# Every engine's queue of a two-layer decoder trunk in an order that a walk over the traced program fixes

## The chip, the cores and the metric

The kernel runs on one core of one Trainium2 chip. The core has several engines that each work through a queue of their own: TensorE (PE) multiplies matrices and transposes, VectorE (DVE) and ScalarE (ACT) work element by element, SyncE (SP) issues most of the DMAs, GpSimd (POOL) does nothing here that counts. An instruction waits at the head of its queue until what it depends on has signalled; what is queued behind it on the same engine waits too. Times are device microseconds (us), and lower is better.

## The reference, cut to what matters

`x` is 256 tokens by 2048. Layer 0 mixes tokens by four causal trailing means (windows 2, 4, 8, 16) with a 512x512 weight for each quarter of the columns; layer 1 by differential attention with 8 heads. Each mixer is followed by a SwiGLU feed-forward part with 5632 inner columns.

```python
for i in range(DEPTH):                       # 2 layers
    hn = rmsnorm(h, norm_mix[i])
    mix = pool_mixer(...) if i % 2 == 0 else diff_attention(...)
    h = h + mix
    h = h + swiglu(rmsnorm(h, norm_ffn[i]), w_gate[i], w_up[i], w_down[i])
return rmsnorm(h, final_norm)

def swiglu(h, wg, wu, wd):
    return (jax.nn.silu(h @ wg) * (h @ wu)) @ wd
```

In the attention a head has two softmaxes, `a = p[0] - lam * p[1]`, and its output `a @ v` is normalised once more before `w_o`.

## The kernel before, in words

All matrices are float32, and each factor of a large product is split in a high and a low part that PE multiplies in its float32r form: high by high, high by low, low by high. `halves` (L118) makes the two parts of a weight tile of four 512-column blocks: `whi` on ACT (L124) and `wlo` on DVE (L125). The weights come by DMAs of 1 MB each, issued by SP (L115), into 3 buffers `raw`; `whi` and `wlo` have 3 buffers each, so the cast to a new `whi` can start only when PE is through with the one three tiles earlier.

The products are made in *groups*. A group takes 8 steps (in w_down 2n of them, n the feed-forward groups of a chunk), one for each pair of 128-row slices of the weight, and sums them in PSUM banks `b0` to `b7`. A plain step makes four blocks of the output with eight products; a *seven* step makes the same with seven products, as in Strassen's and Winograd's scheme, and needs sums of weight blocks (`tsum`, L130 to L133, DVE) and their high and low parts `thi` (L139, ACT) and `tlo` (L140, DVE), as well as sums of the activations (L272 to L277). Steps 2, 4 and 6 are seven steps in most groups. `combined` (L204 to L221) then forms the four output blocks from the banks: copies on ACT (L210, L214) and eight DVE instructions on tiles `c` (L211, L212, L213, L215 to L218, L220), several of which need the one ahead:

```python
nc.vector.tensor_tensor(u2, ps[M6], m1, ALU.add)      # L211
nc.vector.tensor_tensor(u3, ps[M7], u2, ALU.add)      # L213
nc.vector.tensor_tensor(u2, p5, u2, ALU.subtract)     # L215
nc.vector.tensor_tensor(p5, p5, u3, ALU.subtract)     # L216
nc.vector.tensor_tensor(u2, ps[P3], u2, ALU.add)      # L217
```

The stages, in the order in which the program is written: the layer-0 mixer (pool "start"); a feed-forward part with 11 gate-up groups in chunks of 4, 4 and 3, each chunk followed by 2 groups of w_down; four q-and-k groups of two heads each; two v groups of four heads each; two w_o groups; the second feed-forward part; the last normalisation (`finish`).

Behind a gate-up group, ACT applies silu (L486), DVE multiplies gate and up (L487), PE transposes the result in eight 128x128 pieces (L259), and the transposed blocks become `h`, the left factor of w_down. Behind a q-and-k group, ACT scales the blocks (L551), PE transposes them (L607), makes the scores (L576) and, after the softmax on DVE and ACT (L578 to L592), transposes the probabilities `a_sb` (L561). Behind a v group PE multiplies by the probabilities (L622 to L624), a normalisation follows (squares L628 on ACT, `rsqrt` L229 to L234 on DVE with a square root L230 on ACT, scaling L632), and PE transposes `o_n` (L259).

What sets the order: the tile framework takes instructions in the order of the program, weighed by priorities that the code gives at two places (`high_priority(-100)` for one residual, `high_priority(-LATER)` for the last means of the mixer), and puts each engine's instructions into its queue. Work of the next group is written behind what follows a group, but in PE's queue its first products stand among the transposes.

Of the kernel before, what the change touches and what calls it, by code (L numbers as in the profile page):

```python
# [2 lines left out]

# [11 lines left out]
PSUM = bass.MemoryType.PSUM  # L15
# [10 lines left out]
EPS = 1e-6  # L26
WARM = 8
LATER = 70

WINDOWS = (2, 4, 8, 16)  # L30

# [19 lines left out]

A22, A21, A11, A12, S1, S3, S2, S4 = range(8)
T1, T3, T2, T4 = range(4)


@with_exitstack
def trunk_kernel(ctx, tc, x_n, gains, scale_in, final_in, subln, lam_in, band, counts_in, dist,
# [230 lines left out]
    with tc.tile_pool(name="start", bufs=1, reuse_waits="tile") as st:  # L288
# [81 lines left out]
        def scaled_halves(g):  # L370

            y[g] = [st.tile([P, 2, 512], F32R, name="y_hl", bufs=4) for _ in range(2)]
            for t in range(2):
                split(y[g][t], yp[g][t], r_in[:, t:t + 1])

        def means(g):

            zp[g] = [bank(2 + t) for t in range(2)]
            own = lambda t: band_sb[:, g, t * P:(t + 1) * P]
            for j in range(2):  # L380
                nc.tensor.matmul(zp[g][0], own(0), y[g][0][:, j], start=(j == 0), stop=(j == 1))
            for j in range(2):
                nc.tensor.matmul(zp[g][1], own(1), y[g][1][:, j], start=(j == 0), stop=False)
            for j in range(2):
                nc.tensor.matmul(zp[g][1], own(2), y[g][0][:, j], start=False, stop=(j == 1))
# [45 lines left out]
        scaled_halves(3)  # L431
        with tc.high_priority(-LATER):
            means(3)
# [94 lines left out]
    with tc.tile_pool(name="attn", bufs=1, reuse_waits="tile") as ap_, ExitStack() as heads:  # L528
        hq = heads.enter_context(tc.tile_pool(name="qk_sums", bufs=1, reuse_waits="tile"))
        at = heads.enter_context(tc.tile_pool(name="attn_tmp", bufs=2, reuse_waits="tile"))  # L530
# [65 lines left out]
        for g in range(4):  # L596

            order, by_seven = LATE if g else EARLY
# [14 lines left out]
        at = heads.enter_context(tc.tile_pool(name="out_tmp", bufs=2, reuse_waits="tile"))  # L613

        oT = [None] * NP
        for g in range(2):
            order, by_seven = LATE if g else EARLY
# [25 lines left out]
                transposed(xq, j, 4, SEVEN)  # L643

    ffn(1, xq, ss_next, None, None)


def _steps(w, left, right):
# [85 lines left out]
```

## Time and profile before

| | us |
|---|---|
| median of 3 runs | 1836.91 (1836.82 to 1837.41) |
| the profiled execution, its own time | 1837.09 |
| its span, first to last instruction | 1835.3 |
| PE busy | 1823.0 of 1835.3 |
| DVE busy | 1630.5 |
| ACT busy | 1048.7 |

The span is what the profile's records cover; the run's own time lies 1.8 us above. "Busy" for PE means that a matmul or transpose was under way; a weight load (PEld) runs beside it. In a row of the timeline, the first number is the start in us from the span's start, the second how long the row's instructions took from the first one's start to the last one's end, then engine, line, operation, the tile written and the tiles read, their shapes, and how many instructions the row stands for (x6); what stands in brackets is idle time of the engine ahead of it and what ended it. A matmul's duration in such a row (0.39) is longer than the distance from one to the next (0.23), since they are pipelined.

### The profile page before, as it was taken

The numbers are of one execution on the slowest core, as the hardware profiler recorded it, in microseconds if no ns is written. First come the engines' busy times: TensorE is split into PE (matmuls) and PEld (weight loads), VectorE is DVE, ScalarE is ACT, GpSimd is POOL, SyncE is SP. The second block draws the span as 40 slices with busy tenths as digits, with TensorE's granted clock in tenths as the row PEclk, the third lists the DMA queues.
The fourth block names the chain that finished last, engine by engine and source line by source line (L and its number), as shares of the span: only waits on it lengthen the run. The fifth ranks groups of instructions, "written<-read, shape, count | busy, mean of one in ns | idle before, by whom it ended". The sixth has DMA issues, their size and how long they took to land.

```text
span 1835.3 us, 20926 instructions
## 1 busy us (share of the span) xinstructions
PE 1823.0 (99%) x8192; PEld 1492.3 (81%) x8192; DVE 1630.5 (89%) x1692; ACT 1048.7 (57%) x1026; POOL 0.7 (0%) x6
## 2 busy tenths in 40 slices
PE   9999999999999999999999999999999999999997
PEld 6888888888888888888888888888888888888886
DVE  7999999889899899989988789889899899988986
ACT  6655544555554556666667665555554555555563
POOL 0000000000000000000000000000000000000000
PEclk9999999999999999999999999999999999999999
DMA  7555555555555555544554555555555545556552
GB/s 271 200 184 193 208 196 209 204 187 205 205 194 197 205 184 184 206 173 174 182 183 163 181 184 184 206 185 205 204 190 202 207 183 193 212 215 210 202 189 110
DMA packets 50930, 356.35 MB, mean 194 GB/s; under 512 B 6160, under 2 KB 6288, under 8 KB 8464
## 3 DMA queue, kind: packets, MB, share of 16 engines
q1 hardware_dynamic: 49968, 353.40, 53.5%
q10 hardware_dynamic: 864, 1.63, 0.2%
q8 instruction: 64, 1.05, 0.2%
q14 instruction: 34, 0.28, 0.0%
HBM read 352.90 MB, written 2.10 MB: 193 GB/s over the span
## 4 chain that ended last, share of the span: by engine, by line
PE 97%; DVE 1%; ACT 1%; DMA 0%; issue 0%; SPq 0%; DVEq 0%; ACTq 0%
PE b L189 93%; PE b L259 2%; PE b L576 1%; PE b L607 0%; DMA x_tok<-x_n 0%; PE b L368 0%; PE b L624 0%; PE b L622 0%; PE b L623 0%; PE b L561 0%; DVE wlo L354 0%; DVE xt_hl L252 0%; ACT sq L240 0%; DVE wlo L125 0%; DVE z L392 0%
## 5 line engine op out<-in xcount | busy, mean ns | idle before, releaser
L189 PE MATMUL b<-whi,xp 128*128 128x512 f32 x2784 | 899.4, 392 | 0.0
L124 ACT CAST whi<-raw 128x1536 fp32r<-128x1536 f32 (+1 forms) x328 | 578.7, 1764 | 549.6 <-PE b L189 450.4
L125 DVE TENSOR_TENSOR wlo<-raw,whi 128x1536 fp32r<-128x1536 f32 (+1 forms) x328 | 689.6, 2103 | 159.2 <-ACT whi L124 158.9
L189 PEld LDWEIGHTS b<-whi,xp 128*128 128x128 f32 x2784 | 520.1, 188 | 108.2 <-ACT e L272 0.4
L189 PE MATMUL b<-wlo,xp 128*128 128x512 f32 x1392 | 544.2, 391 | 0.0
L189 PE MATMUL b<-whi,h 128*128 128x512 f32 x1108 | 354.2, 390 | 0.0
L189 PEld LDWEIGHTS b<-wlo,xp 128*128 128x128 f32 x1392 | 261.5, 188 | 53.0
L140 DVE TENSOR_TENSOR tlo<-tsum,thi 128x2048 fp32r<-128x2048 f32 x114 | 260.6, 2286 | 8.3 <-ACT thi L139 8.3
L189 PEld LDWEIGHTS b<-whi,h 128*128 128x128 f32 x1108 | 207.5, 188 | 43.2
L139 ACT CAST thi<-tsum 128x2048 fp32r<-128x2048 f32 x114 | 217.6, 1908 | 19.7 <-DVE tsum L133 17.2
L189 PE MATMUL b<-thi,xp 128*128 128x512 f32 x640 | 223.4, 389 | 0.0
L189 PE MATMUL b<-wlo,h 128*128 128x512 f32 x554 | 215.8, 389 | 0.0
L130 DVE TENSOR_TENSOR tsum<-raw 128x1024 f32<-128x1024 f32 x114 | 139.1, 1220 | 2.1 <-DMA raw<-w_v 0.6
L189 PEld LDWEIGHTS b<-thi,xp 128*128 128x128 f32 x640 | 120.1, 188 | 24.7
L189 PE MATMUL b<-tlo,xp 128*128 128x512 f32 x320 | 125.9, 393 | 0.0
L189 PEld LDWEIGHTS b<-wlo,h 128*128 128x128 f32 x554 | 104.0, 188 | 21.3
L189 PE MATMUL b<-thi,h 128*128 128x512 f32 x240 | 83.7, 390 | 0.0
L133 DVE TENSOR_TENSOR tsum<-tsum,raw 128x512 f32<-128x512 f32 x114 | 78.5, 689 | 2.2
L132 DVE TENSOR_TENSOR tsum<-tsum,raw 128x512 f32<-128x512 f32 x114 | 78.1, 685 | 0.6
L189 PEld LDWEIGHTS b<-tlo,xp 128*128 128x128 f32 x320 | 60.0, 188 | 16.5 <-DVE tlo L140 4.4
L189 PE MATMUL b<-whi,oT 128*128 128x512 f32 x216 | 69.7, 395 | 0.0
L189 PEld LDWEIGHTS b<-thi,h 128*128 128x128 f32 x240 | 45.0, 188 | 9.5 <-ACT thi L139 0.4
(147 smaller groups left out, 1211.7 us busy)
## 6 DMA issues: line engine op xcount, KB each, us to landing
raw<-w_gu SPq DMA_DIRECT2D x176, 1024.0 KB, 4.8
raw<-w_down SPq DMA_DIRECT2D x88, 1024.0 KB, 4.8
raw<-w_qk SPq DMA_DIRECT2D x32, 1024.0 KB, 4.8
raw<-w_v SPq DMA_DIRECT2D x16, 1024.0 KB, 4.8
raw<-w_o SPq DMA_DIRECT2D x16, 1024.0 KB, 4.8
x_tok<-x_n SPq DMA_DIRECT2D x4, 512.0 KB, 6.9
w<-pool_w SPq DMA_DIRECT2D x4, 512.0 KB, 7.5
raw<-pool_w SPq DMA_DIRECT2D x2, 1024.0 KB, 11.1
```

The source lines that it names most:

```text
L124: nc.scalar.copy(hi[:, lo_block:], raw[:, lo_block:])
L125: nc.vector.tensor_tensor(lo[:, lo_block:], raw[:, lo_block:], f32(hi[:, lo_block:]), ALU.subtract)
L130: nc.vector.tensor_tensor(t[:, T1:T3 + 1], raw[:, B11:B22 + 1], raw[:, B12:B12 + 1].broadcast_to([P, 2, 512]), ALU.add)
L132: nc.vector.tensor_tensor(t[:, T2], t[:, T1], raw[:, B22], ALU.add)
L133: nc.vector.tensor_tensor(t[:, T4], t[:, T2], raw[:, B21], ALU.add)
L139: nc.scalar.copy(hi, t)
L140: nc.vector.tensor_tensor(lo, t, f32(hi), ALU.subtract)
L189: nc.tensor.matmul(ps[b], x, y[:, block], start=first, stop=(left[b] == 0))
L259: nc.tensor.transpose(ps[:, i, 1 - t if seven else t], src(i, t), ident)
L576: nc.tensor.matmul(sc[:, :nk], qk[:, 0, c, qb * P:(qb + 1) * P], qk[:, 1, c, :nk], start=True, stop=True)
```

## The change

At the end of `trunk_kernel`, when the whole program has been traced, a new function reads the list of instructions, works out which depends on which, gives each a duration by a formula, and walks the program once in the manner of a machine with five queues. Three further walks rank the instructions of DVE and ACT by a due time that is worked out backward from PE's queue (PE's and SP's own are ranked by the order of the program). The queues of PE, DVE, ACT and SP are then tied to the order of the best walk, by an edge from each instruction to the next on its engine. No instruction of PE, DVE or SP is added, taken away or altered; on ACT there are 9 loads of an activation table in place of 7, since functions of different tables now follow each other at two more places.

The diff, cut to its core (`steps_of`, which rebuilds the dependencies from tiles, buffers and pools, is left out but for its head):

```diff
+SIGNAL = 36
+LANDING = 2100
+PER_MIB = 2500
+class Step:
...
+        elif self.engine == PE:
+            n = size(ins.outs[0])
+            one = 110 if ins.is_transpose else 14 + n / 2.4 if "float32r" in str(ins.ins[0].dtype) else 14 + n / 0.6
+            self.holds, self.lasts = one, one + (0 if ins.is_transpose else 60)
+        elif self.engine == DVE:
+            if ins.opcode == "TensorScalarPtr":
+                self.lasts = 185 + n / 0.96 if n > 8 else 159
+            else:
+                self.lasts = 152 + n / (1.92 if ins.opcode == "TensorCopy" else 0.96)
+            self.holds = max(self.lasts - 80, 60)
+        elif self.engine == ACT:
+            self.lasts = 165 + n * 0.852
...
+            self.holds = max(self.lasts - 30, 60)
...
+def steps_of(instructions):
...
+def walk(steps, rank):
...
+    for _ in steps:
+        now, e = min((free[e] if able[e] else max(free[e], coming[e][0][0]), i)
+                     for i, e in enumerate(engines) if able[e] or coming[e])
...
+        s = steps[heapq.heappop(able[e])[1]]
+        start[s.k], free[e] = now, now + s.holds
+        end = now + s.lasts
...
+        for k in s.after:
+            same = steps[k].engine == e and not s.dma
+            ready[k] = max(ready[k], now + s.holds if same else end + SIGNAL)
...
+def due(steps, start):
...
+    for s in reversed(by_start):
+        limit[s.k] = min([limit[k] - s.lasts - SIGNAL for k in s.after] + [at.get(s.k, clock)])
+    return limit
+def in_order_of_need(tc):
+
+    steps = steps_of(list(tc.nc.cur_bb.bb.instructions))
+    rank = [float(s.k) for s in steps]
+    start, end = walk(steps, rank)
+    for _ in range(ROUNDS):
+        limit = due(steps, start)
+        rank = [float(s.k) if s.engine in (PE, SP) else limit[s.k] for s in steps]
+        again, span = walk(steps, rank)
+        if span < end:
+            start, end = again, span
+    order = mybir.DependencyInfo(mybir.DependencyClass.NoSync, mybir.DependencyReason.DATA)
+    for e in (PE, DVE, ACT, SP):
+        line = sorted((s for s in steps if s.engine == e), key=lambda s: start[s.k])
+        for one, two in zip(line, line[1:]):
+            tc.add_manual_dep(two.ins, one.ins.name, order, reason="order of need")
...
     ffn(1, xq, ss_next, None, None)
+    in_order_of_need(tc)
```

The new functions stand at the head of the file, so a line of the changed kernel has a number 167 higher than the same line before (L211 is L378, L487 is L654, L259 is L426, L189 is L356).

What moves, at three places. The first is DVE's queue at the end of the fourth gate-up group of layer 0, from the first recombination of the banks on (`c11` to `c22` are its four tiles, `wlo`, `tsum` belong to weights of the next groups). Before:

```order
L211 TENSOR_TENSOR c12_1698<-b1_1519,c11_1697 128x512
L130 TENSOR_TENSOR tsum_1803<-raw_1801 128x1024
L213 TENSOR_TENSOR c21_1699<-b2_1523,c12_1698 128x512
L212 TENSOR_TENSOR c11_1697<-b6_1440,c11_1697 128x512
L215 TENSOR_TENSOR c12_1698<-c22_1700,c12_1698 128x512
L125 TENSOR_TENSOR wlo_1774<-raw_1771,whi_1773 128x2048
L216 TENSOR_TENSOR c22_1700<-c22_1700,c21_1699 128x512
L217 TENSOR_TENSOR c12_1698<-b4_1447,c12_1698 128x512
L218 TENSOR_TENSOR c21_1699<-b5_1454,c21_1699 128x512
L220 TENSOR_TENSOR c22_1700<-b7_1461,c22_1700 128x512
L487 SCALAR_TENSOR_TENSOR c12_1698<-c12_1698,r_tok_521,c11_1697 128x512
L487 SCALAR_TENSOR_TENSOR c22_1700<-c22_1700,r_tok_521,c21_1699 128x512
```

The same place of DVE's queue in the changed kernel:

```order
L378 TENSOR_TENSOR c12_1698<-b1_1519,c11_1697 128x512
L380 TENSOR_TENSOR c21_1699<-b2_1523,c12_1698 128x512
L382 TENSOR_TENSOR c12_1698<-c22_1700,c12_1698 128x512
L383 TENSOR_TENSOR c22_1700<-c22_1700,c21_1699 128x512
L379 TENSOR_TENSOR c11_1697<-b6_1440,c11_1697 128x512
L292 TENSOR_TENSOR wlo_1774<-raw_1771,whi_1773 128x2048
L384 TENSOR_TENSOR c12_1698<-b4_1447,c12_1698 128x512
L654 SCALAR_TENSOR_TENSOR c12_1698<-c12_1698,r_tok_521,c11_1697 128x512
L385 TENSOR_TENSOR c21_1699<-b5_1454,c21_1699 128x512
L387 TENSOR_TENSOR c22_1700<-b7_1461,c22_1700 128x512
L297 TENSOR_TENSOR tsum_1803<-raw_1801 128x1024
L654 SCALAR_TENSOR_TENSOR c22_1700<-c22_1700,r_tok_521,c21_1699 128x512
```

The first product of gate and up (L654) now stands directly behind the sum that it needs (L384), three places earlier in the queue; the four recombinations ahead follow one another without the sum of weight blocks (`tsum`) between them, which has gone behind. This sequence is the same in 21 of the 22 gate-up groups of the changed kernel.

The second is PE's queue at the same boundary: `b6`, `b4`, `b5` are banks of the next group, `b0` and `b1` receive the transposes. Before:

```order
L189 MATMUL b4_1750<-whi_1739,h_812 128x512 x2
L189 MATMUL b4_1750<-wlo_1740,h_812 128x512
L189 MATMUL b4_1750<-whi_1739,h_812 128x512
L189 MATMUL b5_1757<-whi_1739,h_812 128x512
L189 MATMUL b5_1757<-wlo_1740,h_812 128x512
L189 MATMUL b5_1757<-whi_1739,h_812 128x512
L259 MATMUL b0_1716<-ident_75,c12_1698 128x128
L259 MATMUL b1_1730<-ident_75,c12_1698 128x128
L189 MATMUL b5_1757<-whi_1739,h_812 128x512
L189 MATMUL b5_1757<-wlo_1740,h_812 128x512
L259 MATMUL b0_1716<-ident_75,c22_1700 128x128
L259 MATMUL b0_1716<-ident_75,c12_1698 128x128
```

In the changed kernel:

```order
L356 MATMUL b6_1743<-whi_1739,h_812 128x512
L356 MATMUL b6_1743<-wlo_1740,h_812 128x512
L356 MATMUL b6_1743<-whi_1739,h_812 128x512
L426 MATMUL b0_1716<-ident_75,c12_1698 128x128
L426 MATMUL b1_1730<-ident_75,c12_1698 128x128
L356 MATMUL b6_1743<-whi_1739,h_812 128x512
L356 MATMUL b6_1743<-wlo_1740,h_812 128x512
L356 MATMUL b6_1743<-whi_1739,h_812 128x512
L356 MATMUL b4_1750<-whi_1739,h_812 128x512
L356 MATMUL b4_1750<-wlo_1740,h_812 128x512
L356 MATMUL b4_1750<-whi_1739,h_812 128x512 x2
```

The first two transposes stand behind three products of the next group instead of fifteen; the six others follow after twelve more products, where before two stood between.

The third is PE's queue in the first v group of the attention, at the transposes of the first head's output `o_n` (`whi_7681`, then `whi_7715`, are the weights of the next group's first two steps). Before:

```order
L189 MATMUL b6_7685<-whi_7715,xp_511 128x512 x2
L189 MATMUL b6_7685<-wlo_7716,xp_511 128x512
L189 MATMUL b6_7685<-whi_7715,xp_511 128x512
L189 MATMUL b4_7692<-whi_7715,xp_511 128x512
L189 MATMUL b4_7692<-wlo_7716,xp_511 128x512
L189 MATMUL b4_7692<-whi_7715,xp_511 128x512 x2
L259 MATMUL b2_7574<-ident_75,o_n_7570 128x128
L189 MATMUL b4_7692<-wlo_7716,xp_511 128x512
L259 MATMUL b2_7574<-ident_75,o_n_7570 128x128 x3
```

In the changed kernel:

```order
L791 MATMUL b3_7583<-c21_7535,aT1_5961 128x256
L356 MATMUL b6_7685<-whi_7681,xp_510 128x512
L356 MATMUL b6_7685<-wlo_7682,xp_510 128x512
L356 MATMUL b6_7685<-whi_7681,xp_510 128x512 x2
L356 MATMUL b6_7685<-wlo_7682,xp_510 128x512
L356 MATMUL b6_7685<-whi_7681,xp_510 128x512
L356 MATMUL b4_7692<-whi_7681,xp_510 128x512
L356 MATMUL b4_7692<-wlo_7682,xp_510 128x512
L356 MATMUL b4_7692<-whi_7681,xp_510 128x512 x2
L426 MATMUL b2_7574<-ident_75,o_n_7570 128x128
L356 MATMUL b4_7692<-wlo_7682,xp_510 128x512
L356 MATMUL b4_7692<-whi_7681,xp_510 128x512
```

The transposes of `o_n` have moved forward from the next group's second step into its first: ten products stand between the last product with the probabilities (L791) and the first transpose, where before there were thirty.

More of the change, by code (lines that the diff above doesn't have):

```diff
@@ L1 @@
+import heapq
 import math
@@ L28 @@
 LATER = 70
+ROUNDS = 3
 WINDOWS = (2, 4, 8, 16)
@@ L53, with __init__ @@
 T1, T3, T2, T4 = range(4)
+PE, DVE, ACT, SP, POOL = (mybir.EngineType.PE, mybir.EngineType.DVE, mybir.EngineType.Activation,
+                          mybir.EngineType.SP, mybir.EngineType.Pool)
+SIGNAL = 36
+LANDING = 2100
+PER_MIB = 2500
+class Step:
+    def __init__(self, k, ins=None):
+        self.k, self.ins, self.engine = k, ins, ins.engine if ins else POOL
+        self.dma = bool(ins) and ins.opcode == "DMACopy"
+        self.before, self.after = set(), []
+        if not ins:
+            self.holds = self.lasts = 0
+            return
+        size = lambda ap: math.prod(c for _, c in list(ap.ap)[1:])
+        n = max(size(a) for a in list(ins.outs) + list(ins.ins) if hasattr(a, "ap"))
+        if self.dma:
+            bytes_ = 4 * math.prod(c for _, c in ins.outs[0].ap)
+            self.share = PER_MIB * bytes_ / 2 ** 20
+            self.holds, self.lasts = (60 if self.engine == ACT else 330), LANDING + self.share
+        elif self.engine == PE:
[10 more added lines that the diff above has]
+            self.lasts = 165 + n * 0.852
+            if ins.opcode == "Activation" and any(hasattr(a, "ap") for a in list(ins.ins)[1:]):
+                self.lasts += 100
+            self.holds = max(self.lasts - 30, 60)
+            if len(ins.outs) > 1:
+                self.lasts, self.holds = self.lasts + 190, self.lasts + 160
+        else:
+            self.holds = self.lasts = 400
@@ new lines, in steps_of @@
+def steps_of(instructions):
+    steps, seen, slots, users, gates = [], {}, {}, {}, {}
+    open_, closed, pool_of = [], None, {}
+    for ins in instructions:
+        if ins.opcode == "TilePoolBoundary":
+            if ins.op == "release":
+                past = Step(len(steps))
+                past.before = {k for n in seen if pool_of.get(n) == open_[-1] for k in users[n]}
+                past.before |= {closed} if closed is not None else set()
+                closed = past.k
+                steps.append(past)
+                open_.pop()
+                continue
+            open_.append(len(pool_of))
+            pool_of.update((t.name, open_[-1]) for t in ins.bass_pool_tiles or ())
+            continue
+        if not any(hasattr(a, "bass_ap") for a in ins.outs):
+            continue
+        step = Step(len(steps), ins)
+        for writes, args in ((False, ins.ins), (True, ins.outs)):
+            for a in args:
+                ap = getattr(a, "bass_ap", None)
+                if ap is None or not hasattr(ap.tensor, "tag"):
+                    continue
+                t, dims = ap.tensor, [tuple(d) for d in ap.ap]
+                first = ap.offset % dims[0][0]
+                last = first + sum((c - 1) * s for s, c in dims[1:])
+                alone = writes
+                if t.space == PSUM:
+                    first, last, alone = 0, 511, True
+                if t.name not in seen:
+                    seen[t.name], users[t.name], gate = [], [], set()
+                    line = slots.setdefault(t.tag, [])
+                    bufs = t.bufs or t.tag_meta.bufs
+                    if len(line) >= bufs:
+                        gate.update(users[line[-bufs]])
+                    elif t.name in pool_of and closed is not None:
+                        gate.add(closed)
+                    if line:
+                        gate.add(users[line[-1]][0])
+                    line.append(t.name)
+                    gates[t.name] = gate
+                own = {k for f, l, w, k in seen[t.name] if (w or alone) and f <= last and first <= l}
+                step.before |= own or gates[t.name]
+                if alone:
+                    seen[t.name] = [s for s in seen[t.name] if s[0] < first or s[1] > last or s[3] == step.k]
+                seen[t.name].append((first, last, alone, step.k))
+                users[t.name].append(step.k)
+        step.before.discard(step.k)
+        steps.append(step)
+    for s in steps:
+        for k in s.before:
+            steps[k].after.append(s.k)
+    return steps
@@ new lines, in walk @@
+def walk(steps, rank):
+    missing = [len(s.before) for s in steps]
+    ready, start = [0.0] * len(steps), [0.0] * len(steps)
+    engines = (PE, DVE, ACT, SP, POOL)
+    free, wire = {e: 0.0 for e in engines}, 0.0
+    able, coming = {e: [] for e in engines}, {e: [] for e in engines}
+    for s in steps:
+        if not s.before:
+            heapq.heappush(coming[s.engine], (0.0, s.k))
+    for _ in steps:
+        now, e = min((free[e] if able[e] else max(free[e], coming[e][0][0]), i)
+                     for i, e in enumerate(engines) if able[e] or coming[e])
+        e = engines[e]
+        while coming[e] and coming[e][0][0] <= now:
+            k = heapq.heappop(coming[e])[1]
+            heapq.heappush(able[e], (rank[k], k))
+        s = steps[heapq.heappop(able[e])[1]]
+        start[s.k], free[e] = now, now + s.holds
+        end = now + s.lasts
+        if s.dma:
+            begin = max(now + s.holds, wire)
+            wire = begin + s.share
+            end = begin + s.lasts
+        for k in s.after:
+            same = steps[k].engine == e and not s.dma
+            ready[k] = max(ready[k], now + s.holds if same else end + SIGNAL)
+            missing[k] -= 1
+            if not missing[k]:
+                heapq.heappush(coming[steps[k].engine], (ready[k], k))
+    return start, max(free.values())
@@ new lines, in due @@
+def due(steps, start):
+    by_start = sorted(steps, key=lambda s: start[s.k])
+    at, clock = {}, 0.0
+    for s in by_start:
+        if s.engine == PE:
+            at[s.k], clock = clock, clock + s.holds
+    limit = [0.0] * len(steps)
+    for s in reversed(by_start):
[16 more added lines that the diff above has]
+            tc.add_manual_dep(two.ins, one.ins.name, order, reason="order of need")
+    return start, end, steps
```

## The prediction

> **What bounds the kernel now.** First the page's first part and its chain of work that ended last, by engine:
>
> ```profile
> span 1835.3 us, 20926 instructions
> PE 1823.0 (99%) x8192; PEld 1492.3 (81%) x8192; DVE 1630.5 (89%) x1692; ACT 1048.7 (57%) x1026; POOL 0.7 (0%) x6
> PE 97%; DVE 1%; ACT 1%; DMA 0%; issue 0%; SPq 0%; DVEq 0%; ACTq 0%
> ```
>
> PE is busy for 99% of the span and is 97% of the chain. Then the table by stretches, to see where PE is not busy (columns: stretch, length, busy us of PE, PEld, DVE, ACT, POOL, granted clock, DMA share, GB/s):
>
> ```profile
> 0.00:45.00 45.00, 42.30 (x180) 31.00 (x181) 32.53 (x55) 31.99 (x60) 0.70 (x6) 1.00 0.71 272
> 90.00:750.00 660.00, 660.00 (x2952) 543.12 (x2951) 599.23 (x537) 363.14 (x283) 0.00 (x0) 1.00 0.55 198
> 750.00:980.00 230.00, 230.00 (x1072) 186.60 (x1071) 206.89 (x309) 145.72 (x195) 0.00 (x0) 1.00 0.50 179
> 1085.00:1825.00 740.00, 740.00 (x3305) 609.52 (x3305) 658.88 (x610) 404.01 (x331) 0.00 (x0) 1.00 0.54 194
> ```
>
> The granted clock is 1.00 throughout, and PE has no visible hole in the two feed-forward parts (90 to 750, 1085 to 1825) nor in the attention's q-and-k groups between them. Is it at its rate while it is "busy"? One row of the chain, and two waits with their total, count and longest:
>
> ```profile
> 220.75 124.33 PE b L189 x547
> PEld b L189 <- DVE tlo L140: 6.9, 17, 0.4
> ACT whi L124 <- PE b L189: 450.4, 206, 4.0
> ```
>
> 547 products in 124.33 us are 0.227 us each; I take this as PE's pace, since nothing in the change makes a product shorter. The third row says that the casts of weights wait for PE 206 times, through the three `whi` buffers: DVE and ACT run ahead of PE as far as the buffers let them and then keep its step. So the time can only fall by the few places where PE waits, and it rises by whatever PE meets in its queue before it is ready. The question is not whether urgent steps come earlier, but whether PE's queue now asks for them **sooner than they can come**.
>
> **The feed-forward boundary, 21 identical places.** This is DVE at the end of the fourth gate-up group, and PE beside it:
>
> ```profile
> 207.75 2.29 DVE L125 TENSOR_TENSOR wlo<-raw,whi 128x2048 fp32r<-128x2048 f32 x1 [1.58 <-ACT whi L124]
> 209.96 0.68 DVE L211 TENSOR_TENSOR c<-b,c 128x512 f32<-128x512 f32 x1
> 210.56 1.22 DVE L130 TENSOR_TENSOR tsum<-raw 128x1024 f32<-128x1024 f32 x1
> 211.69 0.68 DVE L213 TENSOR_TENSOR c<-b,c 128x512 f32<-128x512 f32 x1
> 217.50 0.68 DVE L220 TENSOR_TENSOR c<-b,c 128x512 f32<-128x512 f32 x1
> 218.09 1.41 DVE L487 SCALAR_TENSOR_TENSOR c<-c,r_tok,c 128x512 f32<-128x512 f32 x2
> ...
> 216.26 0.62 PE L189 MATMUL b<-whi,h 128*128 128x512 f32 x2
> 219.25 0.38 PE L259 MATMUL b<-ident,c 128*128 128x128 f32 x2
> 219.39 0.48 PE L189 MATMUL b<-whi,h 128*128 128x512 f32 x1
> ```
>
> The first L487 ends at about 218.8, PE needs it at 219.25: 0.4 us in hand. In the changed queue the first two transposes stand twelve products earlier, right behind the product that starts at 216.26, so PE asks at 216.26 + 0.23 = **216.49**. When can the product of gate and up be ready? DVE's new sequence is L211, L213, L215, L216, L212, L125, L217, L487, and the first seven of these stand in that very order in the trace of before, in a q-and-k group:
>
> ```profile
> 831.12 0.68 DVE L211 TENSOR_TENSOR c<-b,c 128x512 f32<-128x512 f32 x1
> 831.91 0.69 DVE L213 TENSOR_TENSOR c<-b,c 128x512 f32<-128x512 f32 x1
> 832.71 0.69 DVE L215 TENSOR_TENSOR c<-c,c 128x512 f32<-128x512 f32 x1
> 833.43 0.69 DVE L216 TENSOR_TENSOR c<-c,c 128x512 f32<-128x512 f32 x1
> 834.64 2.28 DVE L125 TENSOR_TENSOR wlo<-raw,whi 128x2048 fp32r<-128x2048 f32 x1
> 836.84 0.68 DVE L217 TENSOR_TENSOR c<-b,c 128x512 f32<-128x512 f32 x1
> 837.44 0.68 DVE L218 TENSOR_TENSOR c<-b,c 128x512 f32<-128x512 f32 x1
> ```
>
> Here is what the walk leaves out. L218 doesn't need L217 and starts 0.60 behind it; L213 needs L211 and starts 0.79 behind it, L215 again 0.80, though all last 0.68. An instruction that needs its predecessor pays 0.19 more; the walk's rule (`ready = now + holds` on the same engine, holds = 152 + 512/0.96 − 80 = 605 ns) gives it nothing. From L211 to L217 the row gives 5.72. The start of the sequence stays where it is: it is behind a `wlo` that waits for `whi` (1.58 idle), which waits for PE. So L217 at 209.96 + 5.72 = 215.68, L487 0.79 later at 216.47. Its duration, and how soon PE follows DVE, from these rows:
>
> ```profile
> L487 DVE SCALAR_TENSOR_TENSOR c<-c,r_tok,c x44: 740/743/748, 91.8 to 1763.3; 128x512 f32<-128x512 f32 x44
> 22.28 0.74 DVE L252 SCALAR_TENSOR_TENSOR y_hl<-b,r_tok,y_hl 128x512 fp32r<-128x512 f32 x1
> 23.08 0.50 PE L368 MATMUL b<-whi,xt_hl 128*128 128x512 f32 x1 [0.69 <-DVE y_hl L252]
> ```
>
> 216.47 + 0.743 + 0.06 (23.02 to 23.08) = 217.27: **PE stands for 0.78 us.** The second pair: the first L487 holds DVE for 0.67 (1.41 − 0.743), L218 and L220 0.60 each, L130 1.13 (210.56 to 211.69), so the second L487 starts at 219.47 and PE can go on at 220.27; PE, itself late, arrives at 217.27 + 0.14 (219.25 to 219.39) + 2.76 (the twelve products, 216.49 to 219.25) = 220.17. Another 0.10. Sum 0.88 for a group, 21 × 0.88 = **+18.5 us**. PE's lateness isn't won back: it has no idle time afterwards to shorten.
>
> The bounds: if dependent instructions cost nothing extra, the chain is 0.70 shorter (0.19 at L213, 0.20 at L215, 0.12 at L216, 0.19 at L487) and the stall is 0.1; the other way, a `wlo` more ahead of the product would make it 2.2 longer, but the printed order has none. The first gate-up group of layer 0 has another order and is put between 0 and 1; I take 0.
>
> The Trainium skill ("VectorE: DVE Perf Modes", section "The DRAIN you can't avoid") reports eight chained copies at 13.88 us with a semaphore after each and at 13.88 us with one at the end: "the semaphore costs nothing extra here". By it the walk's rule would be right and this term about 2 us. The rows above disagree, 0.79 against 0.60, in this very sequence, so I go by them.
>
> **What goes.** 17 times PE waits for a `tlo` (second row of waits). Once:
>
> ```profile
> 229.71 0.39 PE L189 MATMUL b<-whi,h 128*128 128x512 f32 x1
> 230.09 0.50 PE L189 MATMUL b<-tlo,h 128*128 128x512 f32 x1
> ```
>
> 0.38 between starts instead of 0.227: 0.15 lost. With `tsum` and `tlo` due ahead of the recombined `h` (L277 is put off), these waits should go: 17 × 0.15 = **−2.6 us**. In the mixer two waits stand in the trace, that at 23.08 above (0.69) and this:
>
> ```profile
> 32.98 0.73 PE L368 MATMUL b<-whi,xt_hl 128*128 128x512 f32 x2 [0.62 <-DVE xt_hl L252]
> ```
>
> Together 1.31. Against that, the means and transposes of the last column groups, which filled 53 to 63 us, are taken some 13 us earlier, each behind a chain of dependent small steps; I count some four new waits of 0.2. Net **−0.5**, with −1.3 (none of these) and +1 as bounds. The tail behind the last product keeps its order: 0. SP's queue changes by two small loads: 0.
>
> **Attention.** The same step is taken there: transposes are moved to where the walk thinks they are just ready. What PE waits for there already:
>
> ```profile
> PEld b L607 <- ACT c L551: 2.2, 7, 0.4
> PEld b L561 <- DVE a_sb L592: 2.2, 8, 0.4
> PEld b L259 <- ACT o_n L632: 2.1, 8, 0.4
> ```
>
> These are at most 0.4 each: before is also just in time. In a q-and-k group the transposes of the second `a_sb` now stand about 6.4 us behind the head's scores, where before 10.5 us of PE work lay between; the chain to it has a score sum, a maximum, an exponential, a reciprocal and three dependent steps, and once a `wlo` (2.2 us of DVE). I count 0.4 for the scaled `c`, and 0.6 and 0.8 at two of the four `a_sb` places, less 0.3 that is won back: 1.5 a group, **+6** for four, between 0 and 3 a group (a `wlo` in the way at one place and 0.8 at another).
>
> In the first v group the transposes of the first `o_n` stand 24 products earlier (ten in place of thirty behind the products with the probabilities, which themselves have four fewer among them). Rows of before:
>
> ```profile
> 985.78 1.28 ACT L230 ACT_TABLE_LOAD   x1
> 987.08 0.20 ACT L230 ACTIVATE rs_s<-rs_v 128x2 f32<-128x2 f32 x1
> 989.20 1.91 ACT L139 CAST thi<-tsum 128x2048 fp32r<-128x2048 f32 x1 [1.12 <-DVE tsum L133]
> 991.01 0.83 ACT L632 ACTIVATE o_n<-b,rs_r 128x256 f32<-128x256 f32 x2
> 991.53 0.33 PE L259 MATMUL b<-ident,o_n 128*128 128x128 f32 x1
> ```
>
> PE asks at 991.53 − 24 × 0.227 = 986.1. The table load stays between the squares and the root, and the walk's formulas don't know it. Without the cast (1.91) and DVE's weight sums that delayed it, `o_n` can come at 987.28 (end of the root) + four dependent small steps (some 0.2 each, as the root itself takes, by estimate) + 0.4 (half of 0.83) = 988.5, less 0.5 since the products ahead of it come earlier: PE stands for about 1.9 us. The second head's `o_n` comes behind a `whi` cast (1.9) that PE's queue covers only in part: another 1 us. In the second v group the transposes keep their distance (0 to 1). Sum **+4**, between 0 and 8.
>
> **The sum**, on the profiled run's own time, 1837.1 (1835.3 of span and 1.8 around it; the median of the runs shown is 0.2 lower): 1837.1 + 18.5 − 2.6 − 0.5 + 6 + 4 = **1862.5 us**, 1.4% slower.
>
> **The rivals.**
> - *Only the feed-forward boundary counts*: the attention's chains, freed of what stood between, come in time. 1837.1 + 18.5 − 2.6 − 0.5 = 1852.5. For it: before's waits there are small. Against: the table load.
> - *Waiting instructions on DVE start as soon as independent ones*: the 0.79 would be the q-and-k group's own (another engine's late signal), the products come at 216.57 (217.27 − 0.70), and the stall is 0.1. It decides at a distance of 0.60 against 0.79. Then the waits for `tlo` are won: 1837.1 − 2.6 − 0.5 + 0 to 2 = 1834 to 1836, not slower. More than 1837.1 − 2.6 − 1.3 = 1833.2 can't be won, since no more waits of PE are in the trace.
> - *That, but the attention's chains are late all the same*: 1834 + 10 = 1844.
> - *The attention costs more*: a `wlo` or `whi` stands in each chain's way, or comes late itself behind the chains of four heads. At my upper bounds, 4 × 3 + 8 = 20 in place of 10: 1872.5.
> - *The order changes little*: the framework had the same sequence where it matters, 1837. Against: the printed queues differ at all 21 places.
>
> **How the numbers follow.** Forecast 0.50; feed-forward alone 0.15; attention alone 0.08; more in attention 0.10; not slower 0.13; no effect 0.04. Slower is 0.50 + 0.15 + 0.08 + 0.10 = 0.83. A measurement of this kernel can tell 0.2% (3.7 us) from no change; 1833.2 is just at that bound, so of the other 0.17 I give 0.04 to faster and 0.13 to the same. The range reaches from 1843, under the two cases between, to 1878, which is the heavy case with 0.26 more at each of the 21 places (PE's second wait there at 0.36 in place of 0.10): 0.17 lies below it and some 0.02 above.
>
> **What would show it.** In the profile after, at each gate-up boundary: L654 of the first tile starting 0.79 behind L384, and PEld of L426 waiting about 0.8 us for it, 21 times; L378 to L384 5.7 us apart; the waits for `tlo` gone; at L426 <- `o_n` a wait near 2 us in the first v group; the granted clock still 1.00. If L380 follows L378 at 0.60, or L426 starts without a wait, the main step is wrong; if PE's waits are few and the time is longer all the same, PE's pace of 0.227 has changed, for which no row of before gives a reason.

## The result, and the profile after

The changed kernel takes 1861.68 us (median of 4 runs, 1861.58 to 1861.79) against 1837.03 (1836.82 to 1837.41) for the kernel before on the same chip: a ratio of **1.0134**, 95% interval 1.0116 to 1.0152. It is slower by 24.6 us.

The page of the changed kernel begins like this:

```profile
span 1859.9 us, 20921 instructions
PE 1826.2 (98%) x8192; PEld 1491.1 (80%) x8192; DVE 1659.2 (89%) x1692; ACT 1048.8 (56%) x1028; POOL 0.7 (0%) x6
```

The same instructions on PE, DVE and (but for two table loads) ACT. PE's busy time has grown by 3.2 us (1823.0 before), the span by the 24.6 us. So PE waits more. For whom, the waits say (some rows; who waited for whom, total us, times, longest):

```profile
PEld b L426 <- DVE c L654: 27.6, 43, 1.1
PE b L426 <- DVE c L654: 13.6, 22, 0.7
PEld b L728 <- DVE a_sb L759: 6.1, 13, 0.8
PEld b L426 <- ACT o_n L799: 2.9, 3, 1.6
PEld b L356 <- DVE tlo L307: 1.8, 3, 0.9
PE b L426 <- DVE x_tok L676: 1.9, 2, 1.1
PE b L426 <- DVE x_tok L808: 1.7, 2, 0.9
```

On top stands what was not in this table before: the transposes of the gate-up products (L426, the old L259) wait for L654 (the old L487). PE itself waited there 22 times, at the 21 places and in the first gate-up group; a row of PEld counts the weight loads of both pairs. The waits for `tlo` have gone from 17 to 3. The fourth gate-up boundary, DVE and then PE:

```profile
209.83 0.69 DVE L378 TENSOR_TENSOR c<-b,c 128x512 f32<-128x512 f32 x1
210.62 0.69 DVE L380 TENSOR_TENSOR c<-b,c 128x512 f32<-128x512 f32 x1
215.55 0.69 DVE L384 TENSOR_TENSOR c<-b,c 128x512 f32<-128x512 f32 x1
216.34 0.75 DVE L654 SCALAR_TENSOR_TENSOR c<-c,r_tok,c 128x512 f32<-128x512 f32 x1
...
216.13 0.39 PE L356 MATMUL b<-whi,h 128*128 128x512 f32 x1
217.15 0.44 PE L426 MATMUL b<-ident,c 128*128 128x128 f32 x2 [0.63 <-DVE c L654]
219.97 0.39 PE L356 MATMUL b<-whi,h 128*128 128x512 f32 x1
220.20 0.82 PE L426 MATMUL b<-ident,c 128*128 128x128 f32 x6
```

L378 to L384 takes 5.72, L654 follows 0.79 behind L384, and PE, which could have gone on at 216.13 + 0.23 = 216.36, goes on at 217.15: it stands for 0.79 us (the bracket shows 0.63, since the modelled end of the product before reaches into the gap). The second pair at 220.20 follows its product after 0.23, so nothing is lost there.

Where the 24.6 us lie is seen by comparing the starts of the same numbered product (the 7530 matmuls of L189, or L356) in both traces, stage by stage. This table is worked out from the traces:

```
stage (products)                     after - before, us   in this stage
mixer, to the end of gate-up group 1 (186)     -1.7           -1.7
feed-forward of layer 0 (2990)                 +6.0           +7.7
into the attention (3070)                      +7.2           +1.2
four q-and-k groups (3759)                    +13.1           +5.9
two v groups (4180)                           +16.0           +2.9
two w_o groups, into the second part (4560)   +17.6           +1.6
feed-forward of layer 1 (7529, the last)      +24.6           +7.0
```

### The profile page after: what moved, and what is told of

Read it like the earlier page. It is cut to its first block, busy times and chain, and to the rows that moved or that the text cites. A ratio compares the mean times of both kernels' runs of the same rounds, so it can differ in the third digit from the quotient of the medians.

```text
span 1859.9 us, 20921 instructions
## 1 busy us (share of the span) xinstructions
PE 1826.2 (98%) x8192; PEld 1491.1 (80%) x8192; DVE 1659.2 (89%) x1692; ACT 1048.8 (56%) x1028; POOL 0.7 (0%) x6
## 4 chain that ended last, share of the span: by engine, by line
PE 71%; DVE 18%; issue 6%; ACT 4%; DMA 0%; DVEq 0%; SPq 0%; ACTq 0%
PE b L356 68%; DVE wlo L292 5%; ACT whi L291 3%; PE b L426 2%; DVE c L380 1%; DVE c L382 1%; DVE c L378 1%; DVE c L379 1%; DVE tlo L307 1%; DVE c L654 1%; DVE c L384 1%; DVE tsum L297 1%; PE b L531 1%; DVE s_sb L745 0%; DVE m_neg L747 0%
## 5 line engine op out<-in xcount | busy, mean ns | idle before, releaser
L356 PE MATMUL b<-whi,xp 128*128 128x512 f32 x2784 | 901.6, 392 | 0.0
L356 PEld LDWEIGHTS b<-whi,xp 128*128 128x128 f32 x2784 | 521.6, 188 | 106.2 <-DVE xp L444 0.3
L356 PE MATMUL b<-wlo,xp 128*128 128x512 f32 x1392 | 543.9, 391 | 0.0
L356 PE MATMUL b<-whi,h 128*128 128x512 f32 x1108 | 355.7, 390 | 0.0
L356 PEld LDWEIGHTS b<-wlo,xp 128*128 128x128 f32 x1392 | 261.8, 188 | 52.6
L356 PEld LDWEIGHTS b<-whi,h 128*128 128x128 f32 x1108 | 208.0, 188 | 42.9
L356 PE MATMUL b<-thi,xp 128*128 128x512 f32 x640 | 223.4, 389 | 0.0
L356 PE MATMUL b<-wlo,h 128*128 128x512 f32 x554 | 215.6, 389 | 0.0
L356 PEld LDWEIGHTS b<-thi,xp 128*128 128x128 f32 x640 | 120.1, 188 | 25.2 <-issue 0.3
L356 PE MATMUL b<-tlo,xp 128*128 128x512 f32 x320 | 124.9, 390 | 0.6 <-DVE tlo L307 0.5
L356 PEld LDWEIGHTS b<-wlo,h 128*128 128x128 f32 x554 | 104.1, 188 | 21.2
L356 PE MATMUL b<-thi,h 128*128 128x512 f32 x240 | 83.6, 389 | 0.0
L356 PEld LDWEIGHTS b<-tlo,xp 128*128 128x128 f32 x320 | 60.1, 188 | 14.2 <-DVE tlo L307 1.8
L356 PE MATMUL b<-whi,oT 128*128 128x512 f32 x216 | 69.1, 392 | 0.0
L653 ACT ACTIVATE c<-c,r_tok 128x512 f32<-128x512 f32 x44 | 31.9, 725 | 43.8 <-DVE c L379 36.5
```

The costliest lines, as they stand in the source:

```text
L356: nc.tensor.matmul(ps[b], x, y[:, block], start=first, stop=(left[b] == 0))
L653: nc.scalar.activation(gate, gate, AF.Silu, scale=r[:, t:t + 1])
```

## The experiments

Each kernel is the changed kernel with the edit shown; the walk's rules only decide an order, so all compute the same. The kernel before was timed beside each, 1836.98 to 1837.2 in median.

**1. Gate-up transposes taken later, 400 ns and 1200 ns.** `s.gated` marks VectorE steps that write a tile `c`; the number is 400 or 1200.

```diff
+LATE_BY = 400
...
-            ready[k] = max(ready[k], now + s.holds if same else end + SIGNAL)
+            late = LATE_BY if e == DVE and steps[k].engine == PE and s.gated else 0
+            ready[k] = max(ready[k], now + s.holds if same else end + SIGNAL + late)
```

> The walk is told that a recombined block written by VectorE reaches TensorE 400 ns later than it assumes; nothing else. In the queues only the gate-up transposes move: the first two stand two products further back than in the change, the rest as far behind them as before. Theory 'asked too soon' (PE's queue reaches the transposes 0.79 us before the chain of dependent VectorE steps can deliver): each of 21 waits shrinks by two products, 0.455 us, to about 0.33; 21 x 0.455 = 9.6, so 1861.7 - 9.6 = 1852 us. Rival 'VectorE's own order costs the time' (its queue puts urgent steps ahead of weights that PE then misses): VectorE's order is that of the change, so 1861.7. Rival 'attention makes the loss': 1861.7 too, since the attention is untouched.

> The same with 1200 ns: the first two transposes stand five products (1.14 us) further back than in the change, more than the wait of 0.79. 'Asked too soon': the 21 waits of 0.79 and the small second one (0.05 to 0.1) go entirely, and nothing more is won by the surplus: 1861.7 - 21 x 0.85 = about 1844 us. 'VectorE's own order' and 'attention': 1861.7. If both this and the 400 ns kernel fall in proportion, the price of a place is that of the products between the asking and the delivery.

Measured: **1851.79** (ratio to before 1.0079, 1.0062 to 1.0095) and **1843.81** (1.0035, 1.0022 to 1.0048). The gate-up boundary in the kernel with 400, then in that with 1200:

```profile
216.27 0.44 PE L429 MATMUL b<-ident,c 128*128 128x128 f32 x2 [0.17 <-DVE c L657]
```

```profile
215.61 0.38 PE L429 MATMUL b<-ident,c 128*128 128x128 f32 x2
```

The wait shrinks (from 0.79 to 0.33, between the starts and less PE's pace of 0.23) and then is gone; the times fall by 9.9 and 17.9 us where 9.6 and 17.7 were expected. The rivals, for which nothing moves, are out: 17.9 us of the loss are the 21 places, with the 0.5 of the first gate-up group, whose wait is gone as well.

**2. Only TensorE's queue pinned.**

```diff
-    for e in (PE, DVE, ACT, SP):
+    for e in (PE,):
```

> Only TensorE's queue is tied to the order of the walk; VectorE, ScalarE and SyncE are ordered by the framework, which at the gate-up boundary gives VectorE exactly the sequence of the kernel before. 'Asked too soon': the product now comes as in the kernel before, where it ended at 218.83, 2.34 us behind the place at which PE asks (216.49); with 0.06 for the signal 2.4 us at each of 21 places, 50 us, and some more in the attention: 1885 to 1900 us. 'VectorE's own order costs the time': that order is gone, so about 1837.

Measured: **1962.23** (1.0682, 1.0666 to 1.0698). The direction is that of "asked too soon", and the wait at a boundary is 2.40 us, as worked out:

```profile
187.99 0.39 PE L356 MATMUL b<-whi,xp 128*128 128x512 f32 x1
190.62 0.44 PE L426 MATMUL b<-ident,c 128*128 128x128 f32 x2 [2.24 <-DVE c L654]
```

But the time is 60 us over what was expected. The table by stretches behind this wait shows why (PE busy and its instructions first, the granted clock third from the end):

```profile
190.00:192.00 2.00, 1.38 (x7) 1.21 (x8) 2.00 (x4) 0.06 (x1) 0.00 (x0) 0.99 0.87 369
192.00:195.00 3.00, 3.00 (x8) 2.22 (x8) 2.10 (x2) 0.00 (x0) 0.00 (x0) 0.50 0.00 0
195.00:197.00 2.00, 2.00 (x12) 1.72 (x11) 0.51 (x2) 1.23 (x4) 0.00 (x0) 0.91 0.93 262
```

For some 3 us after the wait the clock was 0.50, and 8 products took what else 13 take. In this execution 71.7 us ran at 0.50, up to the last product; as an estimate that costs at most half of them, 36 us. With 50 for the 21 places that leaves some 39 of the 125 us for longer waits in the attention and the mixer, where I had expected only some. The step that failed in this expectation is the clock, which was not in it at all.

**3. The price of dependent VectorE steps told to the walk.**

```diff
+CHAINED = 110
...
-            ready[k] = max(ready[k], now + s.holds if same else end + SIGNAL)
+            ready[k] = max(ready[k], (end + CHAINED if e == DVE else now + s.holds) if same else end + SIGNAL)
```

> One rule of the walk is corrected: a VectorE step that needs an earlier VectorE step is ready 110 ns after that one's end (for 512 columns 0.79 us from start to start, as the trace has it), no longer at its 'holds' (0.60). The walk then puts the first transposes six products ahead of where they stood before (217.87 in the old time) and not twelve, and weaves a sum of weights into the chain. By hand the product comes at 217.9 there: no wait. 'Asked too soon, through the price of dependent steps': the 21 waits go (-17.9), much of the attention's waits goes too (its transposes stand further back, at most places behind where they were before), the table load stays: 1834 to 1841 us, middle 1837. If dependent steps are not the cause, the walk's places stay too early and at least 1850 remains.

Measured: **1832.30** (0.9974, 0.9963 to 0.9984): 29.4 us under the change, and faster than the kernel before. At the gate-up boundary:

```profile
213.46 0.68 DVE L385 TENSOR_TENSOR c<-b,c 128x512 f32<-128x512 f32 x1
214.06 0.68 DVE L384 TENSOR_TENSOR c<-c,c 128x512 f32<-128x512 f32 x1
214.66 0.74 DVE L655 SCALAR_TENSOR_TENSOR c<-c,r_tok,c 128x512 f32<-128x512 f32 x1
...
215.19 0.39 PE L357 MATMUL b<-whi,h 128*128 128x512 f32 x1
215.46 0.44 PE L427 MATMUL b<-ident,c 128*128 128x128 f32 x2
```

The walk now weaves an independent step between two that depend on each other, the starts lie 0.60 apart, and PE takes the transposes 0.27 after the product ahead of them, where 0.23 is its pace. With one rule of the walk corrected the whole loss is gone, in the attention as well: from product 3070 to 4560 this kernel loses nothing against before (−3.1 there, −3.9 at the end), where the change lost 10.4.

**4. Table loads told to the walk**, without experiment 3. Silu, exponential and square root belong to three tables; a change between them adds 1283 ns.

```diff
+SETS = {AF.Silu: 1, AF.Exp: 2, AF.Sqrt: 3}
+LOAD = 1283
...
+        need = SETS.get(getattr(s.ins, "func", None), table) if e == ACT and s.ins.opcode == "Activation" else table
+        load = LOAD if need != table else 0
+        table = need
+        start[s.k], free[e] = now, now + s.holds + load
+        end = now + s.lasts + load
...
-            ready[k] = max(ready[k], now + s.holds if same else end + SIGNAL)
+            ready[k] = max(ready[k], free[e] if same else end + SIGNAL)
```

> The change, with the walk told that ScalarE spends 1.283 us on loading a table where a square root, an exponential or a silu follows another of the three; the price of dependent VectorE steps stays as in the change. In the queues the transposes of the first v group's outputs stand 6 products (1.36 us) and 21 products later than in the change, and the first gate-up group's 5 later; the 21 other gate-up places are the same. If the table load makes the waits there (1.30 and 0.54 in the v group, 0.53 at the first gate-up group in the profile of the change), they go: 1861.7 - 2.4 = 1859.3 us. If the v group's chain is late for another reason, 1861 to 1862. In neither case does the large loss move.

Measured: **1860.57** (1.0128, 1.0114 to 1.0142), 1.1 us under the change and half of what was expected. The two ratios to before overlap in their intervals, so the traces are the firmer evidence. The v group's two waits, in the profile of the change

```profile
998.41 1.28 ACT L397 ACT_TABLE_LOAD   x1
1001.25 0.33 PE L426 MATMUL b<-ident,o_n 128*128 128x128 f32 x1 [1.14 <-ACT o_n L799]
```

are gone, and 0.2 of the first gate-up group's 0.5; what was not foreseen are 0.34 more at two gate-up places and at one later `o_n`. So the v group's waits go when the walk knows of the table load, which stands in the chain ahead of `o_n`; but it is a small part, and asking as much later for another reason would have taken them too.

**5. The other half: VectorE, ScalarE and SyncE pinned, TensorE not.**

```diff
-    for e in (PE, DVE, ACT, SP):
+    for e in (DVE, ACT, SP):
```

> VectorE, ScalarE and SyncE are tied to the order of the walk, TensorE is not: the framework orders PE, and puts the first gate-up transposes 9 products ahead of where they stood before (the change: 12), at 217.18 in the old time, when the product is ready at 217.27. 'Asked too soon': the wait there is 0.1, 21 x 0.1 = +2; the waits for tlo (-2.9) and those in the mixer (-1.6) are won as in the change; attention between none and half of the change's 8: 1835 to 1841, middle 1837. 'VectorE's own order costs the time': 1855 or more, as the loss would stay with that order.

Measured: **1845.46** (1.0048, 1.0035 to 1.006), above the expected range. The feed-forward parts came out as expected (by the starts of the same products −0.7 together), but in the mixer and the attention PE, in the framework's order, meets products that the pinned queues don't serve in time. The largest stand three times in the q-and-k groups, 1.75 us and twice 2.0 over PE's pace; this is the first:

```profile
841.15 0.47 PE L356 MATMUL b<-whi,xp 128*128 128x512 f32 x1 [1.59 <-DVE c L379]
```

L379 (the old L212) empties a bank. The walk puts it behind four dependent steps (here a `wlo` of 2.28 us stands ahead of it as well), and the framework's PE queue has the next product into that bank at once. Behind the third of these waits the granted clock is 0.50 for 3.4 us, up to another 1.7 us. So VectorE's order isn't free of cost by itself; it costs where PE's order wasn't made with it. Neither half of the change alone is as fast as the kernel before.

**6. Both corrections, then a reserve.** `chain_table` has the edits of 3 and 4; the others have a reserve for PE's waits in addition (300, 600 or 900 ns; `spare900` and `chain_spare` leave out what their names leave out).

```diff
+SPARE = 300
...
-            ready[k] = max(ready[k], (end + CHAINED if e == DVE else free[e]) if same else end + SIGNAL)
+            ready[k] = max(ready[k], (end + CHAINED if e == DVE else free[e]) if same else end + SIGNAL + (SPARE if steps[k].engine == PE else 0))
```

> Both corrections of the walk together: dependent VectorE steps at 110 ns behind the end, and the table loads. Against the kernel with the first correction alone (1832.3) the transposes of the first v group stand 13 to 29 products later and the first gate-up group's 6 later; there it still waited 0.89 and 0.73. Both should go: 1832.3 - 1.6 = 1830.7 us. If instead what is put behind the table load comes late elsewhere, 1832 to 1834.

> The same, and each PE step that waits for another engine is taken to be ready 300 ns later than the walk works out, as a reserve. PE's remaining waits are small (under 0.2 each); if they are misjudged arrivals, the reserve removes some: 1830 to 1830.7. If they are PE's own (changes between its forms of product), nothing moves: 1830.7. A loss would show that transposes put off too long make the left factors of later products late.

> The change with one number: every PE step that waits for another engine is taken to be ready 900 ns later than the walk works out. Neither the price of dependent VectorE steps nor the table load is corrected. 'Asked too soon': the 21 gate-up places stand four products (0.9 us) further back than in the change, which covers 0.79 + 0.1 (-18); most of the attention's waits (under 0.6 each) and the new ones at the transposes of x (1.23 and 1.02) go as far as 0.9 covers them; the v group keeps some 0.5: 1861.7 - 18 - 8 = 1835 us, between 1832 and 1839. If the attention loses through VectorE's own order, 1840 to 1844.

> The price of dependent VectorE steps and 300 ns of reserve for PE, without the table load. Against the fastest kernel so far (1829.3, all three) only the table load is missing; 300 ns don't cover 1.283, but the queues show the first v group's transposes 19 to 26 products behind their place before, so no wait there: 1829 to 1831 us. 'The table load is needed': 1831 to 1833.

> All three, with twice the reserve. If the reserve only has to cover what the walk misjudges, 300 were enough and 600 gives the same 1829.3 (within 0.7). If putting off transposes makes the left factors of later products late, it is slower, 1831 or more; the kernel with 300 waits three times at products in the attention (0.56, 1.00 and 0.78), which could grow.

```
kernel                 median us   ratio to before (95%)      expected
chain_table             1839.90    1.0016 (1.0006 to 1.0025)   1830.7
chain_table_spare       1829.27    0.9958 (0.9946 to 0.9971)   1830 to 1830.7
spare900                1834.55    0.9986 (0.9978 to 0.9995)   1835
chain_spare             1836.76    0.9998 (0.9990 to 1.0007)   1829 to 1831
chain_table_spare600    1837.56    1.0004 (0.9995 to 1.0013)   1829.3
```

`spare900` says the same as experiment 1 for the whole program: without any corrected price, merely asking later takes 27.1 us off the change. `chain_table_spare` is the fastest of all, 0.42% under the kernel before. Three came out worse than expected. In `chain_table` the waits of the v group are gone, but others have come, the largest 0.9 in the mixer and 1.3 at the first product of the attention, and the waits for `tlo` that the change had removed are back, more of them than before:

```profile
PEld b L364 <- DVE tlo L315: 9.8, 28, 0.7
```

With truer prices the walk found another order, not one that is better everywhere; why it puts `tlo` late there was not followed up. In `chain_spare` and `chain_table_spare600` transposes of the probabilities are put off so far that something behind them comes late. ACT and PE of `chain_spare` at the probabilities of the third q-and-k group, among the fourth's products:

```profile
922.08 0.37 ACT L731 COPY aT<-b 128x256 f32<-128x256 f32 x1 [3.76 <-PE b L730]
922.50 1.92 ACT L293 CAST whi<-raw 128x2048 fp32r<-128x2048 f32 x1
924.31 1.91 ACT L308 CAST thi<-tsum 128x2048 fp32r<-128x2048 f32 x1
...
926.27 1.26 PE L358 MATMUL b<-thi,xp 128*128 128x512 f32 x4 [1.93 <-ACT thi L308]
929.00 0.80 PE L358 MATMUL b<-tlo,xp 128*128 128x512 f32 x1 [1.47 <-DVE tlo L309]
```

ACT stands for 3.76 us at the head of its queue for the transposed probabilities; the casts behind it are late, PE waits 1.9 and 1.5 for them, and its clock is 0.50 for 6.8 us from 927.3 on. In `chain_table_spare600` the same copy stands for 3.23 us at those of the first, and 10.2 us of the profiled execution ran at 0.50. Its eleven runs differ more than those of the other kernels (1835.99 to 1841.5), and the time goes with the granted clock: 0.998 or 0.999 up to 1836.4, 0.997 about 1837.5, 0.995 from 1840.5 on. So its median says little about the reserve itself beyond that it no longer helps. A reserve helped here only as long as nothing that PE needed was queued behind a step that waited for PE.

## Why the prediction was right, point by point

1862.5 was forecast, 1861.7 measured. The terms, by the table of stages and the runs:

- **Gate-up boundary, +18.5.** Measured 0.79 at each of 21 places, 16.6; taking the transposes later won 17.9 (experiment 1, with the first gate-up group). The first wait came out as worked out (0.78); of the second (0.10) nothing came, as PE took 2.86 us from the first of the twelve products to the second transposes (217.34 to 220.20) in place of the 2.76 in the sum, and L654 was done by then (219.34 + 0.75, by the timeline). The mechanism, a dependent step 0.79 behind its predecessor where the walk has 0.60, stands in the rows above, and experiment 3 shows that telling the walk of it takes the loss away. The sentence of the Trainium skill ("VectorE: DVE Perf Modes", section "The DRAIN you can't avoid") that a semaphore costs nothing extra doesn't describe this sequence: 0.79 again in the changed kernel, L378 to L380. Whether the semaphore or the wait for the written tile costs the 0.19, no run here separates.
- **The waits for `tlo`, −2.6.** 17 waits became 3. Both feed-forward parts together grew by 14.7; with 16.6 for the 21 places, 0.5 for the first gate-up group, which I had put at 0, and 1.0 for transposes of x (below), 3.4 were won back. The term is of the right size; what else was won there was not followed up.
- **Mixer, −0.5.** Measured −1.7, outside my bound of −1.3 too. I had counted four new waits of 0.2 against the 1.3 that goes; most of these did not come, at least not at that size (one of 0.38 stands at 56.04). An undersized gain; what was won beyond the 1.3 was not followed up.
- **q-and-k groups, +6.** Measured +5.9, by waits of 0.3 to 0.6 at the scaled `c`, the scores and `a_sb`. They go with the price of dependent steps (experiment 3: −0.8 in these groups); a reserve of 900 ns without that price leaves 2.9 of them.
- **v groups, +4.** Measured +2.9: 0.55 at the products with the probabilities, 1.30 and 0.54 at the first two heads (1.9 and 1 forecast). The table load of 1.28 stands ahead of the first of them, and both go in experiment 4.
- **Left out altogether: the transposes of x** at the end of layer 0's last w_down group and of the two w_o groups, +2.8 (1.2 and 1.6 in the table): waits of 1.23, 1.02 and 0.97, less what was won between. One more of 0.98, at 719.01, lies in the feed-forward part of layer 0. Before, PE has no such wait there. Here too the walk has them too early, behind a chain in which each sum with x (L676, in w_o L808) needs the step just ahead; DVE, then PE, at the first of the three:

```profile
751.97 0.68 DVE L385 TENSOR_TENSOR c<-b,c 128x512 f32<-128x512 f32 x1
752.68 0.69 DVE L676 TENSOR_TENSOR x_tok<-c,x_tok 128x512 f32<-128x512 f32 x1
...
753.43 1.09 PE L426 MATMUL b<-ident,x_tok 128*128 128x128 f32 x8 [1.07 <-DVE x_tok L676]
```

I had put the w_down and w_o groups at nothing because their banks come free in time, and had not looked at their transposes. This miss of 2.8, and those of the other terms in the other direction (feed-forward 1.2, mixer 1.2, v groups 1.1, together 3.5), nearly cancel. That the sum is closer than its parts is luck; the mechanism and its largest term are not.

The rival that was not slower needed 0.60 between dependent steps, and the trace has 0.79. The rival with attention unchanged missed 5.9 + 2.9. That transposes put far off can make weights late (the heavier rival) hardly happened in the change (one wait of 0.64 for a `tlo`, at 838.85), but did in two experiments.

One bound was wrong: the prediction let nothing be won below 1833.2, since no more waits of PE stood in the trace. The kernel of experiment 3 (1832.30) and `chain_table_spare` (1829.27) lie below it. By the starts of the same products, the latter wins 3.0 us against before in the mixer and 5.1 in the two feed-forward parts, where the prediction had counted 1.3 and 2.6. So the kernel before lost more in small gaps than the waits counted; which ones was not followed up.

## What to carry to other kernels

Where one engine is busy all the time and takes its queue in order, a place in that queue is a promise of an arrival time: in this kernel being too early cost the whole difference, at every repetition, and being somewhat too late cost nothing until something else ran out. An order worked out from durations therefore has to know what the last steps ahead of that engine really cost, or to keep some reserve at each hand-over: the price of dependent steps alone took off 29.4 us, a plain reserve of 900 ns 27.1. But a truer price or a longer reserve is no sure gain, since the walk then finds another order: the table load's price won 1.1 us alone and lost 7.6 on top of the first price, and a reserve stopped paying where a waiting step had work for the same engine queued behind it. With one queue pinned to the plan and the others not, both halves of this change were slower than the kernel before.

## What the runs showed of the hardware that was not expected

TensorE's clock halves after waits that are shorter than I would have thought. The records of the clock show that its changes lie on a fixed grid of 3.413 us. Adding up PE's waits in each cell of that grid (worked out from the trace of the kernel with only PE pinned: gaps of more than 0.05 us beyond the usual distance to the next instruction, cells at full clock):

```
waits in one cell of 3.41 us     cells   next cell at clock 0.50
up to 1.99                        528    0
2.06 to 2.13                        4    1
2.15 and more                      17   17
```

What is taken as the usual distance moves a cell's sum by up to 0.1, so the border lies somewhere between 2.0 and 2.2 us. The other kernels agree: four of their cells, with 2.08 (experiment 5), 2.20 (`chain_spare`), 2.50 and 2.48 (`chain_table_spare600`), were each followed by half the clock, and no other cell of theirs reaches 1.9. Whether the clock counts a transpose as work was not separated.

So of the 21 equal waits of 2.40 us at gate-up boundaries only 9 were followed by half the clock. That at 190.62 above lies for the most part in one cell, which ends at 191.96; that at 237.09 is cut by the border at 236.33 into 1.64 and 0.76, and the clock behind it is 1.00. A halved cell costs up to another 1.7 us, half of its length. In the changed kernel no cell has more than 1.5, and its clock stays at 1.00. The Trainium skill ("TensorE: Matmul & The Clock Gate", section "What's actually happening") gives the grid: a free-running window of 3413 ns, with which these records agree. It names a whole idle window as the condition, and under "Why this matters for your kernels" it warns of gaps above some 3 us; here a little over 2 us within one window was enough.
